# Half of an adaLN modulation as products on TensorE, and the output gate moved into the weights: a hybrid attention and state-space layer on one core

## The chip, the cores and the metric

The kernel runs on one core of one Trainium2 chip. The metric is the device time of one execution in microseconds (us); the runs shown are three. Engines: PE (TensorE, with its weight loads as PEld), DVE (VectorE), ACT (ScalarE), POOL (GpSimd), and SP, whose queue issues most of the transfers. Each engine takes its instructions in the order in which the program holds them. "Line" is a line of the kernel before; lines behind 235 lie 35 to 42 further down in the changed kernel.

## What is computed

One layer on 1024 tokens of width 1024, batch 1, all in float32:

```python
mod = jax.nn.silu(c) @ w_ada + b_ada                 # c: 1024, w_ada: 1024 x 3072
shift, scale, gate = jnp.split(mod, 3, axis=-1)
h = rms_norm(x, norm_g) * (1 + scale) + shift
proj = h @ w_in                                      # 1024 x 2840, split into
q, kcr, vcr, ksl, vsl, kwn, vwn, z_a, g_br, u, z_s = jnp.split(proj, offs, axis=-1)
attn = nsa_attention(...) * silu(z_a)                # 8 heads: compressed, selected, window branch
y = gelu(s5_mixer(u, ...))                           # diagonal state space, 32 groups of 64 states
ssm = y * sigmoid(y @ glu_w + glu_b) * silu(z_s)
mix = jnp.concatenate([attn, ssm], axis=-1) @ w_out  # 1024 x 1024
return x + gate * mix
```

So `shift` and `scale` are needed before any projection, `gate` only at the end, and `gate` runs along the columns of `w_out`.

## The kernel before

The program is a list of named steps in `ORD`; `I(name, *deps)` (line 1348) binds a name to a function and to the steps that must stand ahead of it, and the loop at line 1556 calls them in the order of `ORD`. The framework then lays down each engine's instructions; in the first part VectorE, ScalarE and SP keep the order of the list. `FLG` says on which engine a step's pass runs: "d" VectorE, "p" GpSimd, "a" ScalarE, "t" an accumulating transfer.

Start. `mod_chunk(j)` (line 230) loads 128 columns of `w_ada`, transposed, as 128x1024, multiplies them by silu(c) in one pass `wada<-wada,sc` on VectorE and sums along the row into one column of `macc`. Sixteen chunks make shift (`mb0` to `mb7`) and scale (`ma0` to `ma7`), eight more the gate (`mod0` to `mod7`, later). `mod_cols(k)` turns two sums into the columns `gs`, `sh` of chunk k. `x_block` transposes a chunk of the scaled x into PSUM (`ptr`), `h_chunk` (line 290) writes it as a high part `hhi` and a float32 copy `hf` on ScalarE, and the low part `hlo`. All projections are three products of high and low parts of h and the weights: `TProj` (`kva0` to `kva7`, PSUM `ptp`, weights `wsp` loaded as `wraw`) and `c_proj` (PSUM `pcp`; `pu` for the S5 input, weights `wh`, `wl`).

Middle (50 to 300 us): key, value, query projections, S5 passes, compression. From 300 to 440 us: the first four tiles of 128 queries, eight heads each (scores `S`, probabilities `pp`, their float16 high and low parts `hl`, transposed by SP's DMA transposes into `PT`, products with V in `po`), between the products of the z paths.

End (from 440 us): the GLU writes the S5 branch into `ps`; `gate_row` (line 1026) spreads the gate over 128 partitions; `wout` (line 1035) loads a block of `w_out` as `wor` and splits it into `wo`. `ssm_out(i)` (line 1063) multiplies the S5 half of tile i by its rows of `w_out`, and for each half of 512 columns VectorE makes two passes: PSUM times 0.125 times gate, and an add of x (`xo`; for tile 2 GpSimd's queue adds x by a transfer). Between them run the tiles 7, 6, 5, 4 of the attention. `attn_out` and `last_out` end in `out_half` (line 1306), again two passes: `o<-po,gate` and `o<-o,ps`, and the store.

## Time and profile before

| | |
|---|---|
| Runs | 694.77, 694.79 and 696.99 us, median 694.79 |
| Profiled execution | 691.38 us, of which the span (first to last instruction) is 689.5 us |
| Mean granted clock of TensorE | 0.980 of full speed |
| Busy, PE / DVE / ACT / POOL | 623.5 / 567.3 / 377.9 / 148.6 us |
| Transfers | 116.76 MB, mean 169 GB/s |

Durations below come from the one profiled execution. A busy PE counts any time in which a product is under way, so products with gaps in their flow count too. The chain of waits follows the last instruction back, at each step to what released it.

### The profile page before, as it was taken

What the parts mean: (1) busy time and instruction counts of PE and PEld (TensorE: products, weight loads), DVE (VectorE), ACT (ScalarE), POOL (GpSimd) and SP (SyncE); (2) the same over time, 40 slices, a digit from 0 to 9 for tenths busy, and PEclk for the clock granted to TensorE, in tenths of its full rate; (3) what the DMA queues carried; (4) which work ended last, traced back from release to release, by engine and by line L of the source; (5) the groups of instructions that cost most, each with busy time, mean ns of one, the idle gap of its engine ahead of it and who ended that gap; (6) DMA issues with size and microseconds to landing.
All of it is one profiled execution on the core that took longest, in us unless ns stands there. A gap on an engine that the chain in (4) does not pass through costs nothing.

```text
span 689.5 us, 12618 instructions
## 1 busy us (share of the span) xinstructions
PE 623.5 (90%) x4662; PEld 492.1 (71%) x4662; DVE 567.3 (82%) x1106; ACT 377.9 (55%) x732; POOL 148.6 (22%) x159
## 2 busy tenths in 40 slices
PE   2478999999698999999999999989899999799996
PEld 0356787788587886888788887556677777687775
DVE  5998999777937889876677787998898998998872
ACT  3677413735162252555586786547756855756640
POOL 0153209147232020640011101132001220011010
PEclk9989999999899999999999999999999999999999
DMA  8975211355276624373656868499689599688994
GB/s 319 417 246 104 47 62 41 115 158 136 64 246 199 212 68 109 83 231 94 131 139 154 207 186 183 124 207 208 183 172 206 132 226 222 184 215 213 224 222 86
DMA packets 209759, 116.76 MB, mean 169 GB/s; under 512 B 159073, under 2 KB 188513, under 8 KB 209698
## 3 DMA queue, kind: packets, MB, share of 16 engines
q1 hardware_dynamic: 205858, 109.38, 61.5%
q0 software_dynamic: 3840, 6.57, 4.0%
q8 instruction: 37, 0.61, 0.3%
q14 instruction: 24, 0.20, 0.1%
HBM read 58.10 MB, written 18.61 MB: 111 GB/s over the span
## 4 chain that ended last, share of the span: by engine, by line
PE 41%; DVE 21%; issue 5%; ACT 4%; DMA 2%; SPq 1%; POOL 1%; DVEq 0%; ACTq 0%; POOLq 0%
PE pcp L351 9%; PE po L1053 8%; PE S L1170 7%; DVE hl L148 4%; PE po L1263 3%; PE pglu L1015 3%; DVE st L1187 3%; PE ptp L331 2%; PE ptp L332 2%; PE ptp L330 1%; DVE ps L151 1%; ACT pp L1203 1%; DVE z L151 1%; PE pg L530 1%; PE ph L901 1%
## 5 line engine op out<-in xcount | busy, mean ns | idle before, releaser
L1203 ACT ACTIVATE pp<-S,st 128x640 f32<-128x640 f32 (+7 forms) x128 | 88.6, 699 | 60.5 <-DVE st L1187 46.5
L148 DVE SCALAR_TENSOR_TENSOR hl<-pp,st,hl 128x640 f16<-128x640 f32 (+7 forms) x128 | 100.5, 817 | 4.9 <-ACT hl L1222 4.8
L1222 ACT ACTIVATE hl<-pp,st 128x640 f16<-128x640 f32 (+7 forms) x128 | 85.2, 728 | 8.2 <-DVE st L151 7.1
L1053 PE MATMUL po<-wo,oh 128*128 128x512 f32 x264 | 85.2, 407 | 3.7 <-DVE wo L151 2.4
L351 PE MATMUL pcp<-hhi,wh 128*128 128x512 f32 x208 | 84.8, 408 | 0.0
L351 PE MATMUL pcp<-hhi,wl 128*128 128x512 f32 x208 | 82.6, 397 | 0.0
L351 PE MATMUL pcp<-hlo,wh 128*128 128x512 f32 x208 | 82.4, 396 | 0.0
L1187 DVE TENSOR_REDUCE st<-S 128x1 f32<-128x1024 f32 (+3 forms) x64 | 57.5, 916 | 6.9 <-PE S L1170 6.7
L1170 PE MATMUL S<-kT,qh 128*128 128x128 f32 (+3 forms) x192 | 60.7, 375 | 1.0 <-ACT pp L1203 0.7
L1053 PEld LDWEIGHTS po<-wo,oh 128*128 128x128 f32 x264 | 48.7, 191 | 14.9 <-DVE wo L151 3.8
L330 PE MATMUL ptp<-wsp,hhi 128*128 128x512 f32 x128 | 53.5, 420 | 6.5 <-ACT hhi L296 4.1
L1263 PE MATMUL po<-V,PT 128*128 128x64 f16 x1584 | 59.0, 193 | 0.0
L1263 PEld LDWEIGHTS <-PT 128*128 128x128 f16 x1584 | 54.0, 98 | 5.7 <-issue 5.1
L1170 PE MATMUL S<-kT,ql 128*128 128x128 f32 (+3 forms) x192 | 55.3, 346 | 0.1
L332 PE MATMUL ptp<-wsp,hlo 128*128 128x512 f32 x128 | 53.0, 416 | 1.5 <-POOL hlo L151 1.5
L331 PE MATMUL ptp<-wsp,hhi 128*128 128x512 f32 x128 | 53.5, 418 | 0.5 <-DVE wsp L151 0.5
L151 POOL TENSOR_TENSOR qr<-ropeb 128x512 f32<-128x512 f32 x16 | 23.5, 1488 | 121.7 <-DVE ropeb L151 69.7
L1053 PE MATMUL po<-wo,ol 128*128 128x512 f32 x120 | 47.9, 402 | 0.8 <-DVE ol L151 0.8
L1170 PEld LDWEIGHTS S<-kT,qh 128*128 128x128 f32 x192 | 33.7, 193 | 17.2 <-issue 11.8
L351 PEld LDWEIGHTS pcp<-hlo,wh 128*128 128x128 f32 x208 | 39.1, 188 | 9.2
L351 PEld LDWEIGHTS pcp<-hhi,wh 128*128 128x128 f32 x208 | 39.2, 189 | 8.3
L351 PEld LDWEIGHTS pcp<-hhi,wl 128*128 128x128 f32 x208 | 39.2, 188 | 8.1
(327 smaller groups left out, 1351.5 us busy)
## 6 DMA issues: line engine op xcount, KB each, us to landing
wada<-in_w_adaT_dram SPq DMA_DIRECT2D x24, 512.0 KB, 6.6
wr<-in_w_in_dram SPq DMA_DIRECT2D x14, 512.0 KB, 4.5
x<-in_x_dram SPq DMA_DIRECT2D x8, 512.0 KB, 6.8
wor<-in_w_out_dram SPq DMA_DIRECT2D x8, 512.0 KB, 4.5
out_dram<-o SPq DMA_DIRECT2D x16, 256.0 KB, 2.5
wraw<-in_w_in_dram SPq DMA_DIRECT2D x15, 256.0 KB, 4.7
xo<-in_x_dram SPq DMA_DIRECT2D x14, 256.0 KB, 3.4
ud<-U SPq DMA_DIRECT2D x4, 512.0 KB, 3.2
```

Source lines behind the costliest of these rows:

```text
L148: dve.scalar_tensor_tensor(out=o, in0=a, scalar=s, in1=b, op0=o0, op1=o1, **kw)
L151: e.tensor_tensor(out=o, in0=a, in1=b, op=op)
L330: pe.matmul(p, H(k)[:, tsl], w[:, 0, :], start=k == 0, stop=False)
L331: pe.matmul(p, H(k)[:, tsl], w[:, 1, :], start=False, stop=False)
L332: pe.matmul(p, H(k, True)[:, tsl], w[:, 0, :], start=False, stop=k == 7)
L351: pe.matmul(p[:], w[:, k, :], H(k, l)[:, halves(half)], start=(k == 0 and w is hi and not l), stop=(k == 7 and l))
L1053: pe.matmul(p, a[x][:, k, :], w[y][:, halves(n)], start=k == 0 and m == 0, stop=k == 3 and m == 2)
L1170: pe.matmul(R[:, c0:c1], w, x, start=bank not in opened, stop=False, skip_group_check=True)
L1187: dve.tensor_reduce(out=st[br], in_=us[br][0][:, :W], axis=AX.X, op=OP.max, negate=True)
L1203: act.activation(pp[:, :W], R[:, :W], AF.Exp, bias=st[br], accum_out=st4[:, 1, 2 * (h % 2) + br:2 * (h % 2) + br + 1])
L1222: act.activation(hl[:, :W], pp[:, :W], AF.Copy, scale=st[br])
L1263: pe.matmul(o, p, v, start=first, stop=end, skip_group_check=True)
```

## The change

Four things change. (1) Columns 0 to 511 of shift and scale (chunks k = 0 to 3) come from TensorE: `w_ada` is laid out as two groups of 128x4096, loaded in four pieces of 512 KB each (`wan`), and 16 products with one stationary column of silu(c) and 512 moving columns sum into a row `pga`; the row is copied and turned into four columns by four small products (`pgc`), and one or two passes write `gs` or `sh`. Chunks 4 to 7 stay as they were. (2) `gate_row` comes before the first heads, and `wprep(k)` loads each of the eight blocks of `w_out`, multiplies it by the gate (six on VectorE, two on GpSimd) and writes it to a DRAM tile `wd`; `wout` loads from there. (3) `ssm_out` and `out_half` leave PSUM in one pass each; x is loaded for all tiles. (4) `ORD` and `FLG` are new.

```diff
 ORD = """
-sc1 sc0 lb pu xl_0 sq0 sq2 sq1 sq3 ma7 mb4 ma0 rstd0 mb0 kvaw0 ma5 xl_1 xsc0 sq5 xb10 sq4 xb00 sq6 sq7 mg mc0 h00 mb2
+sc1 scT lb mg gl00 xl_0 sq2 gl10 gl11 sc0 sq1 gl01 sq3 ga00 ga10 ga01 gl02 ga02 sq0 gl03 ga03 rstd0 xsc0 gc0 ga11 gl12
...
+    sc2 = macc[:, 0:16].rearrange("p (a k) -> p a k", a=2)[:, :, 0:4]
+    def sc_cols():
+        cT = w2([128, 2, 4], F32, "cT")
+        dma(cT[:].rearrange("p a k -> p (a k)"), t["cT"])
+        act.activation(sc2, cT[:], AF.Tanh, scale=0.5)
+        stt(sc2, sc2, 1.0, cT[:], OP.add, OP.mult)
+    def ada_load(g, q):
+        GR[g, q] = w = w4([128, 2, 512], F32, "wan")
+        dma(w[:].rearrange("p a n -> p (a n)"), t["w_adaN"][g, :, 1024 * q:1024 * q + 1024], "m")
+    def ada_mms(g, q):
+        if q == 0:
+            GR[g] = ppv("pga")
+        w = GR.pop((g, q))
+        for m in range(2):
+            k = 2 * q + m
+            pe.matmul(GR[g][0:1, :], macc[:, k + k // 4 * 4:k + k // 4 * 4 + 1], w[:, m, :], start=k == 0, stop=k == 7)
+    def ada_cols(g):
+        row = w2([1, 512], F32, "row")
+        act.copy(row[:], GR.pop(g)[0:1, :])
+        p = ppv("pgc")
+        for n in range(4):
+            pe.matmul(p[:, n:n + 1], row[0:1, n * 128:(n + 1) * 128], ident[0:1, 0:1], start=n == 0, stop=n == 3, skip_group_check=True)
+        if g:
+            stt(sh[:, 0:4], p[:, 0:4], 0.5, bada[:, 0:4], OP.mult, OP.add)
+        else:
+            tt(dve, gs[:, 0:4], p[:, 0:4], hng[:, 0, 0:4], OP.mult)
+            tt(dve, gs[:, 0:4], gs[:, 0:4], hng[:, 1, 0:4], OP.add)
...
+    wd = [dram.tile([128, 1024], F32, name=f"wd{k}") for k in range(8)]
     def gate_row():
-        M["gate"] = gate = cur["f2"].tile([128, 1024], F32, name="gate")
+        M["gate"] = gate = w4([128, 1024], F32, "gate")
...
+    def wprep(k):
+        w = w4([128, 1024], F32, "wog")
+        dma(w[:], t["w_out"][128 * k:128 * k + 128, :], "o")
+        tt({"p": pool, "d": dve}[FLG.get(f"wg{k}", "d")], w[:], w[:], M["gate"][:], OP.mult)
+        dma(wd[k][:], w[:], "W")
     def wout(half, k):
...
-            dma(raw[:], t["w_out"][r0:r0 + 128, :], "o")
+        dma(raw[:], wd[4 * half + k][:], "o")
...
-            stt(ps[:, i, halves(n)], p[:], 0.125, M["gate"][:, halves(n)], OP.mult, OP.mult)
-            on = FLG.get(f"xa{i}", "d")
-            if on != "t":
-                xo = f2([128, 512], F32, "xo")
-                dma(xo[:], xr[:, i, halves(n)], "i")
-                tt({"p": pool, "d": dve}[on], ps[:, i, halves(n)], ps[:, i, halves(n)], xo[:], OP.add)
-        if on == "t":
-            pool.dma_start(ps[:, i, :], xr[:, i, :], accum_op=OP.add)
+            xo = f2([128, 512], F32, "xo")
+            dma(xo[:], xr[:, i, halves(n)], "i")
+            stt(ps[:, i, halves(n)], p[:], 0.125, xo[:], OP.mult, OP.add)
...
-        tt(dve, o[:], p[:], M["gate"][:, halves(n)], OP.mult)
-        on = FLG.get(f"ao{i}{n}", "d")
-        if on == "t":
-            pool.dma_start(o[:], r, accum_op=OP.add)
-        else:
-            tt({"p": pool, "d": dve}[on], o[:], o[:], r, OP.add)
+        tt(dve, o[:], p[:], r, OP.add)
...
-            I(f"h{k}{h}", f"mc{k}", f"xb{k}{h}")(
+            I(f"h{k}{h}", *((f"mc{k}",) if k >= 4 else ("gc0", "gc1")), f"xb{k}{h}")(
...
-    I("grow", "sp", "modf")(gate_row)
+    I("grow", "modf")(gate_row)
+    for k in range(8):
+        I(f"wp{k}", "grow", *([f"wp{k - 1}"] if k else []))(lambda k=k: wprep(k))
```

How the instructions stand now, at four places. ScalarE in the first part, before, from its third row on (`x_72` and `x_73` are the halves of x, `hhi_91` the high part of the chunks 0 to 3):

```order
L242 ACTIVATE sq,ss<-x_72 128x1024 x2
L208 CAST wsp<-wraw 128x512
L257 ACTIVATE x_72<-x_72,rstd 128x1024 x2
L242 ACTIVATE sq,ss<-x_73 128x1024 x4
L296 ACTIVATE hhi_91<-ptr,sh,gs 128x512
L296 ACTIVATE hf<-ptr,sh,gs 128x512
L257 ACTIVATE x_73<-x_73,rstd 128x1024 x2
```

And after, from the second copy of a row `pga` on:

```order
L260 COPY row<-pga 1x512
L208 CAST wsp<-wraw 128x512
L331 ACTIVATE hhi_91<-ptr,sh,gs 128x512
L331 ACTIVATE hf<-ptr,sh,gs 128x512
L277 ACTIVATE sq,ss<-x_73 128x1024 x3
L331 ACTIVATE hhi_91<-ptr,sh,gs 128x512
L331 ACTIVATE hf<-ptr,sh,gs 128x512
L292 ACTIVATE x_73<-x_73,rstd 128x1024 x2
L208 CAST wsp<-wraw 128x512
```

The first `hhi` stood behind four squares of the second half of x; now it stands behind one of them, two copies of `pga` and two casts, and three squares stand behind it. From here to the last of three casts `wh<-wr` follow five more passes `hhi` and `hf` of other chunks.

PE's first rows, before:

```order
L224 MATMUL pcb<-cr,ones 128x512 x2
L265 MATMUL ptr<-ident,x_72 128x128 x8
L330 MATMUL ptp<-wsp,hhi_91 128x512
L331 MATMUL ptp<-wsp,hhi_91 128x512
L332 MATMUL ptp<-wsp,hlo_93 128x512
```

And after:

```order
L224 MATMUL pcb<-cr,ones 128x512 x2
L255 MATMUL pga<-wan,macc 1x512 x11
L263 MATMUL pgc<-ident,row 128x1 x4
L255 MATMUL pga<-wan,macc 1x512 x5
L263 MATMUL pgc<-ident,row 128x1 x4
L300 MATMUL ptr<-ident,x_72 128x128 x12
L365 MATMUL ptp<-wsp,hhi_91 128x512
```

The 16 products `pga` and two groups of four small ones now stand ahead of the first transpose of x, and 12 transposes instead of 8 ahead of the first product `ptp`.

SP from 337 us on, when the second tile's probabilities are transposed, before (`wr`, `ad`, `zsd`, `py` are other transfers of that stage):

```order
L1246 DMA_TRANSPOSE PT<-hl 128x4x128 x4
L140 DMA wr_3357<-in_w_in_dram 128x8x128
L140 DMA ad_130<-A 128x512
L140 DMA zsd_125<-zz 128x1024
L140 DMA py__3506<-yd_114 128x512
L1246 DMA_TRANSPOSE PT<-hl 128x4x128 x10
```

And after, at about the same heads:

```order
L140 DMA wog<-in_w_out_dram 128x1024
L1280 DMA_TRANSPOSE PT<-hl 128x4x128 x4
L140 DMA wd_135<-wog 128x1024
L1280 DMA_TRANSPOSE PT<-hl 128x4x128 x4
L140 DMA wog<-in_w_out_dram 128x1024
L1280 DMA_TRANSPOSE PT<-hl 128x4x128 x2
L140 DMA wr_3805<-in_w_in_dram 128x8x128
L140 DMA wd_136<-wog 128x1024
L1280 DMA_TRANSPOSE PT<-hl 128x4x128 x2
```

Loads `wog` and writes `wd` of 512 KB now stand between the transposes; a write waits for its product with the gate, and what is behind it on SP waits too.

VectorE's last rows, before:

```order
L148 SCALAR_TENSOR_TENSOR za<-za,vsc,pat 128x256
L151 TENSOR_TENSOR oh<-za,oh 128x256
L151 TENSOR_TENSOR o<-po,gate 128x512
L151 TENSOR_TENSOR o<-o,ps 128x512
L151 TENSOR_TENSOR o<-po,gate 128x512
L151 TENSOR_TENSOR o<-o,ps 128x512
```

And after:

```order
L148 SCALAR_TENSOR_TENSOR za<-za,vsc,pat 128x256
L151 TENSOR_TENSOR oh<-za,oh 128x256
L151 TENSOR_TENSOR o<-po,ps 128x512 x2
```

Of the two passes of each half one is left.

## Rows read from the trace of the kernel before

**Rows 1.** Stages: us, busy time per engine, PE clock, DMA share, GB/s.

```profile
50.00:300.00 250.00, 234.95 (x1304) 191.81 (x1303) 209.15 (x519) 108.11 (x194) 84.22 (x103) 0.98 0.43 122
300.00:440.00 140.00, 138.47 (x1007) 108.07 (x1006) 104.52 (x199) 93.92 (x246) 19.83 (x20) 1.00 0.65 162
475.00:675.00 200.00, 186.57 (x1960) 151.91 (x1960) 179.94 (x258) 126.19 (x216) 26.25 (x19) 0.98 0.89 199
675.00:689.50 14.50, 8.47 (x127) 6.59 (x125) 3.65 (x6) 0.79 (x2) 0.00 (x0) 1.00 0.30 75
```

**Rows 2.** The chain that ended last, from 475 us on, shares by line.

```profile
by line: PE po L1053 26.5%; PE S L1170 11.5%; DVE hl L148 10.7%; issue 8.6%; DVE st L1187 7.9%; PE po L1263 6.1%; DVE ps L151 3.3%; DVE wo L151 3.2%; DVE o L151 3.2%; DVE ps L148 1.9%; ACT pp L1203 1.9%; DMA PT<-hl 1.7%; DVE za L148 1.4%; A
```

**Rows 3.** Stages of the first 50 us.

```profile
0.00:10.00 10.00, 3.75 (x4) 1.16 (x4) 2.98 (x8) 3.44 (x4) 0.66 (x6) 1.00 0.78 259
10.00:20.00 10.00, 0.00 (x0) 0.00 (x0) 9.02 (x23) 3.13 (x7) 1.27 (x1) 1.00 1.04 406
20.00:30.00 10.00, 5.38 (x15) 3.72 (x16) 8.63 (x26) 7.92 (x13) 1.29 (x1) 1.00 1.03 419
30.00:40.00 10.00, 6.10 (x23) 3.85 (x23) 9.69 (x18) 6.44 (x10) 4.94 (x3) 0.83 1.08 382
40.00:50.00 10.00, 8.29 (x33) 6.09 (x34) 9.05 (x16) 7.48 (x11) 3.39 (x3) 0.83 0.59 181
```

**Rows 4.** VectorE's groups by shape: busy us, mean ns, idle before, releaser.

```profile
L148 DVE SCALAR_TENSOR_TENSOR wada<-wada,sc 128x1024 f32<-128x1024 f32 x24 | 32.6, 1369 | 7.8 <-DMA wada<-in_w_adaT_dram 7.8
...
L151 DVE TENSOR_TENSOR o<-o,ps 128x512 f32<-128x512 f32 x16 | 10.9, 686 | 0.2
...
L151 DVE TENSOR_TENSOR ps<-ps,xo 128x512 f32<-128x512 f32 x14 | 10.2, 732 | 0.1
...
L151 DVE TENSOR_TENSOR wo<-wor,wo 128x1024 fp32r<-128x1024 f32 x8 | 9.6, 1216 | 0.1
```

**Rows 5.** Instructions of the tail in time: start, us, engine and line.

```profile
680.00 0.38 ACT L1279 ACTIVATE A<-po 128x256 f32<-128x256 f32 x1 [6.20 <-PE po L1263]
...
680.91 0.48 DVE L148 SCALAR_TENSOR_TENSOR za<-za,vsc,pat 128x256 f32<-128x256 f32 x1 [6.66 <-PE pat L1333]
...
685.72 0.69 DVE L151 TENSOR_TENSOR o<-o,ps 128x512 f32<-128x512 f32 x1
```

**Rows 6.** GpSimd's groups by shape.

```profile
L151 POOL TENSOR_TENSOR qr<-ropeb 128x512 f32<-128x512 f32 x16 | 23.5, 1488 | 121.7 <-DVE ropeb L151 69.7 <-DVE vs L157 21.9 <-issue 16.4
```

**Rows 7.** Transfers by line: size and us to landing.

```profile
wor<-in_w_out_dram SPq DMA_DIRECT2D x8, 512.0 KB, 4.5
...
PT<-hl SPq DMA_TRANSPOSE x120, 3.5
```

**Rows 8.** The chain that ended last, PE's long pieces.

```profile
445.07 10.37 PE pglu L1015 x24
...
512.26 5.58 PE po L1053 x24
```

**Rows 9.** The start in time.

```profile
2.33 3.75 PE L224 MATMUL pcb<-cr,ones 1*128 1x512 f32 x4 [2.33 <-DMA cr<-in_c_dram]
...
24.97 0.76 ACT L296 ACTIVATE hhi<-ptr,sh,gs 128x512 fp32r<-128x512 f32 x1
...
25.79 0.80 PE L330 MATMUL ptp<-wsp,hhi 128*128 128x512 f32 x1 [2.17 <-ACT hhi L296]
...
50.78 0.73 PE L351 MATMUL pu<-hhi,wh 128*128 128x512 f32 x2 [0.28 <-ACT wh L208]
...
63.74 0.40 PE L330 MATMUL ptp<-wsp,hhi 128*128 128x512 f32 x1
```

**Rows 10.** ScalarE's groups by shape, first 60 us.

```profile
L296 ACT ACTIVATE hhi<-ptr,sh,gs 128x512 fp32r<-128x512 f32 x10 | 7.8, 777 | 7.5 <-PE ptr L265 4.8 <-DVE sh L157 2.2 <-DVE gs L157 0.5
...
L242 ACT ACTIVATE sq<-x 128x1024 f32<-128x1024 f32 x6 | 6.3, 1044 | 2.3 <-DMA x<-in_x_dram 2.3
...
L208 ACT CAST wsp<-wraw 128x512 fp32r<-128x512 f32 x7 | 4.1, 614 | 4.8 <-DMA wraw<-in_w_in_dram 4.8
L208 ACT CAST wh<-wr 128x1024 fp32r<-128x1024 f32 x3 | 3.0, 1038 | 0.0
```

More of the change, by code (lines that the diff above doesn't have):

```diff
@@ L1386, in hymba @@
     I("lb")(lb)
+    I("scT")(sc_cols)
+    for g in range(2):
+        for q in range(4):
+            I(f"gl{g}{q}")(lambda g=g, q=q: ada_load(g, q))
+            I(f"ga{g}{q}", f"gl{g}{q}", "scT", *([f"ga{g}{q - 1}"] if q else []))(lambda g=g, q=q: ada_mms(g, q))
+        I(f"gc{g}", f"ga{g}3", "mg")(lambda g=g: ada_cols(g))
     I("mg", "lb")(mod_gains)
@@ L1572, in arrange @@
     a["w_adaT"] = g("w_ada").T
+    a["w_adaN"] = np.stack([np.ascontiguousarray(g("w_ada")[:, o:o + 512]).reshape(8, 128, 512).transpose(1, 0, 2).reshape(128, 4096)
+                            for o in (1024, 0)])
+    a["cT"] = g("c").reshape(8, 128).T
     a["b_ada"] = g("b_ada").reshape(24, 128).T
```

89 lines of the change are left out of this document (43 added, 46 removed).

## The prediction, made before the changed kernel was run

> **What bounds the kernel now.** I read the table of stages first [rows 1]. In each stage compare PE's busy time with the length of the stage, then VectorE's. From 300 to 440 us PE is busy for 138.47 of 140 us (98.9%): nothing taken off another engine there is worth anything. From 475 to 675 us PE is busy for 186.57 of 200 us (93.3%) and VectorE for 179.94 (90.0%): two engines near their limits that wait for each other, with 13.4 us of idle PE. The tail from 675 us has PE busy for 8.47 of 14.5 us. From 50 to 300 us PE is idle for 15.05 of 250 us. Second, the chain of waits from 475 us on [rows 2]: PE's products lead it, but VectorE's passes are links too, among them `ps` on L151 (3.3%) and `o` on L151 (3.2%), which are the passes at issue. Third, the first 50 us in steps of ten [rows 3]: PE is busy for 23.52 of 50 us, and between 10 and 40 us the DMA engines are full (share 1.03 to 1.08, near 400 GB/s). PE waits there for the weights of the modulation, and for VectorE, which reduces them and is busy for 9.69 us between 30 and 40 us.
>
> **The change part by part.**
>
> *Adds removed.* Each of the 16 half tiles of the last stage loses one add `o<-o,ps`, and 14 of the 16 halves of `ssm_out` lose `ps<-ps,xo`; the multiply that stays turns into the add, in one pass of the same shape. By the groups of VectorE [rows 4] this is 16 x 0.686 = 11.0 us and 14 x 0.732 = 10.2 us, 21.2 us together, all behind the GLU. (The two halves of tile 2 exchange one accumulating transfer of GpSimd's queue for two loads on SP, priced at nothing: such loads are there for the other 14.) What that is worth I take in two ways. (a) Compare stages: from 300 to 440 us VectorE is 74.7% busy and PE 98.9%; from 475 to 675 us 90.0% and 93.3% [rows 1]. So 15.3 points of VectorE go with 5.6 points of PE, 0.37 points per point. Two of the adds lie in the tail; the other 28 are 19.8 us of 179.94. With 160.1 us of VectorE and a stage of 194.5 us its share is 82.3%, PE's share by that slope 96.1%, and 186.57 / 0.961 = 194.1 us: it closes at about 194, a gain of 6. (b) Count in the chain: `ps` and `o` on L151 are 6.5% of the 214.5 us from 475 us to the end, 13.9 us [rows 2]. All `o` on L151 are two passes per half, of which one goes, so half of 3.2% counts, 3.4 us. In `ps` on L151 a part belongs to the GLU product, which stays; if two thirds are the adds, 4.7 us. That is 8 us. In the tail the last add (685.72, 0.69 us) stands behind the last multiply with nothing beside it [rows 5] and goes whole: 0.7 us. I take 7 us with the tail. Bounds: 0, if other waits end last in the same places, and 13.4 + 1.4 = 14.8 us, if all idle PE of the stage and two passes of the tail go.
>
> *Gate into the weights.* `wprep` adds eight products of 128x1024, six on VectorE and two on GpSimd, and 16 transfers of 512 KB. The nearest row of VectorE is `wo<-wor,wo` of that size, 1.216 us [rows 4]: 7.3 us more between about 300 and 400 us, where VectorE is 74.7% busy. They lie beside PE's z products; uncovered they would cost 7.3 us. On GpSimd, two passes of 128x512 with fp32 operands take 2 x 1.488 us [rows 6], so some 3 us for each product, on an engine that is busy for 19.83 of 140 us. `gate_row` with its eight transposes and two copies only moves, from the stage with idle PE into one without; I put 1 us on that. The transfers add 8.4 MB to 140 us at 162 GB/s, 22.7 MB [rows 1]: 37% more, or the share 0.65 turned to 0.89. A load of 512 KB lands after 4.5 us, a transpose of probabilities after 3.5 us [rows 7]. Each write of `wd` waits on SP for its product, and SP holds the transposes of P behind it, for which PE waits in turn. I take nothing for these waits beside the 1 us, as the order has several products of z ahead of them on PE; bounds 0 and 8 us (eight writes, each late by 1 us).
>
> *Modulation on TensorE.* Eight passes `wada<-wada,sc` go from VectorE's first 45 us, 8 x 1.369 = 11 us [rows 4]. The bytes are the same, so what the DMA sets stays. New are 16 fp32 products with 512 columns, and a rule that no first chunk of `h` starts before both halves of four columns are done; before, chunk 0 needed two weight chunks. On PE a fp32 product of 512 columns is two records. At the high clock 24 records took 10.37 us [rows 8], 0.43 us each; the four of `pcb` took 3.75 us at the low one, 0.94 each [rows 9]. The first `wan` chunk ends at 2.7 MB of traffic (2.1 of x and 0.1 of small loads stand ahead of its 0.5). With 2.6 MB in the first 10 us and 4.1 MB in the next ten [rows 3] that is 10.2 us, and the eighth (6.75 MB) is in at 20.2 us. If PE is at the high level behind the first two products, the 32 records take 4 x 0.94 + 28 x 0.43 = 15.8 us and end at 26.0 us: PE, not the DMA, sets this end. The column step (copy, transposing products, a pass of VectorE) is like 680.00 to 681.39 us in the tail, 1.4 us [rows 5], and half a microsecond of the first group's step lies inside: 28 us. So the first `hhi` comes 3 us later than today's 24.97 [rows 9].
> Then it has to be made up. In the new order ACT has nine `hhi`/`hf` (0.775 us), three squares and two scalings (about 1.04), one cast of 0.61 and three of 1.04 us up to the third `wh` [rows 10], 15.9 us, and I add 2.5 us of waits for `rstd1` and its PSUM tiles, an estimate: 46.5 us. The first product of `pu` starts there against 50.78 today [rows 9]. Today 12 more products of `ptp` are done by then, 12 x 0.233 us by the row of 24 in 5.58 us [rows 8], 2.8 us. Ahead by 1.5 us there; behind it PE has 54 products up to k=4, 12.6 us, and some 3 us of transposes and waits for ACT, an estimate. Both orders have the same products ahead of k=4, which starts at 63.74 us today [rows 9] and at about 62 us by this count. I take a gain of 2 us, with bounds of +6 (the first 45 us of VectorE were the wait) and -12 (the low clock, below).
>
> *The rest of the order* from 50 to 300 us: PE is idle for 15 us, which is the upper bound of a gain; a loss of the same size in waits for S5 can't be ruled out. The S5 passes on VectorE start at much the same time by my count (they follow the same casts), so I take 0, with 4 us to either side.
>
> **Sum.** -7 (adds, with the tail) + 1 (middle) - 2 (start) + 0 = -8 us. The profiled execution spans 689.5 us and was timed at 691.4; the median of the runs is 694.8, 3.4 above it. The difference is carried over: 681.5 us of span, 683.4 profiled, 686.8 as a median. I say 686.5.
>
> **The rivals.**
> *Low clock at the start (ends slower).* Each pair of `pga` products waits for a transfer of its own. If PE stays at 1.2 GHz through the `pga` products, the 32 records take 30.1 us instead of 15.8, the columns come at 42 instead of 28 us, and everything behind them on ACT shifts, since the order keeps ACT's `hhi` in line: 14 us lost, 700.5 us. It decides once the products end behind about 38 us. For it: PE's granted clock fell to 0.83 in the mean between 30 and 50 us, when PE was busy for 6 to 8 of 10 us [rows 3]. Against it: PE would have its next chunk waiting at any time after 12 us, as each pair takes longer (1.7 us at the high level) than the transfer of its chunk (1.3 us at 406 GB/s).
> The Trainium skill ("TensorE: Matmul & The Clock Gate", "Loop structure matters more than you think") warns of just this form, a wait for a DMA between products, after which PE runs cold; by that rule the time is the 700 us of this rival. Trace and rule agree on the fall between 30 and 50 us, but no row before shows products of this shape, so the chance stays small.
> *The writes hold up SP (no gain).* The 16 transfers and the waits for products delay transposes from 300 to 440 us by the 8 us of the bound; 686.5 + 7 = 693.5 us. For it: SP issues in order, and the share of DMA rises to 0.89. Against: from 475 us on the share is 0.89 as well, and PE still gets 93.3% [rows 1].
> *VectorE was the whole wait.* Idle PE in the last stage goes to a third: a gain of 13.4 x 2/3 + 1.4 = 10.3 us there, 4 at the start, and 3 from the middle, where S5 starts earlier: 694.8 - 17.3 + 1 = 678.5 us. For it: VectorE is 90% busy and its passes come right behind one another. Against: 600 to 675 us is also full of scores that wait for ACT.
> *The adds were hidden anyway.* The removed passes ran while PE worked; the gain is the tail's 0.7 and the start's 2: 693 us.
>
> **Chances.** Forecast (681 to 692) 0.50; low clock 0.13; SP 0.12; all of VectorE 0.17; hidden 0.08. A difference below 0.3% (2.1 us) can't be told from none here. Faster: 0.48 of the forecast, 0.17, and a third of SP and hidden, 0.07: 0.72. Same: 0.02 + the rest of these two, 0.13: 0.15. Slower: 0.13. The range takes in the forecast, VectorE's case and the lower part of the low clock: 675 to 698.
>
> **What would show it.** In the trace after: VectorE some 15 us below its old busy time from 475 us to the end and PE at 96% there; no passes `o<-o,ps`; the last copy out one pass earlier. At the start: 32 `pga` records with a spacing near 0.43 us, ending at about 26 us, the first `hhi` near 28 us and `pu` near 46.5. From 300 to 440 us PE still at 98% or more. I am wrong if the `pga` records are spaced by more than 0.8 us, if PE's share from 300 to 440 us falls below 96%, or if PE's share from 475 us on stays at 93%.

## The result, and the profile after

The changed kernel takes 701.2 us (median of 16 runs, 696.7 to 704.3) where the kernel before takes 694.8 (16 runs, 690.8 to 697.0): ratio 1.0088, 95% interval 1.0064 to 1.0113. It is slower by 0.9%. The prediction was 686.5 us, range 675 to 698.

The profiled execution of the changed kernel spans 701.7 us, 12.2 more than that of before. To see where they come in, take five events that both kernels have and read their start times from the groups of instructions of each tile: the first score product (`S`), the last product of the z columns (`pcp`), the last GLU product (`pglu`), the last pass that takes a half of the S5 output out of PSUM (`ps<-po`) and the last pass that writes a result (`o`). All are in us; "again" is a second profile of the same kernel.

```
                      before   again   after   again   before -> after   predicted
start to first S       299.5   300.7   307.3   309.0        +7.8          -2 + 0
first S to last pcp    121.3   120.5   131.5   131.0       +10.2          +1
last pcp to last pglu   52.5    53.8    54.2    54.5        +1.7           0
last pglu to last ps   114.7   113.3   105.8   105.5        -8.9       } -7 in both
last ps to last o       97.7    97.8    98.8    98.8        +1.1       }
```

The lines of the first score product and of the last z product, before and then after:

```profile
L1170 PE MATMUL S<-kT,qh x192: 220/395/776, 299.5 to 656.4; 128*128 128x512 f32 x88, 128*128 128x128 f32 x56, 128*128 128x256 f32 x24, 128*128 128x384 f32 x24
...
L351 PE MATMUL pcp<-hlo,wh x208: 392/396/477, 105.5 to 420.8; 128*128 128x512 f32 x104
```

```profile
L1204 PE MATMUL S<-kT,qh x192: 220/392/735, 307.3 to 668.2; 128*128 128x512 f32 x88, 128*128 128x128 f32 x56, 128*128 128x256 f32 x24, 128*128 128x384 f32 x24
...
L386 PE MATMUL pcp<-hlo,wh x208: 387/396/480, 105.0 to 438.8; 128*128 128x512 f32 x104
```

The second profiles repeat every stretch within 1.7 us. But the profiled executions differ by more than the kernels do: they were timed at 691.4 us (3.4 under the median of before) and 703.5 us (2.3 over the median of after), 12.1 us apart, where the medians are 6.4 apart; the second ones, at 691.8 and 704.6 us, lie on the same sides. So the table holds some 6 us that the medians don't have. From the first score to the timed end each kernel takes nearly the same in its two profiles (391.9 and 391.1 us before, 396.2 and 395.6 after). If that also holds at the medians, the first score comes at about 303.3 us before and 305.3 after, an estimate: a loss of about 2 us there and not 7.8. The section on how far one profile can be trusted comes back to this.

The gain is there, in the place where it was expected. One loss far beyond what was expected comes ahead of it, from 300 to 440 us, and one before 300 us whose size is open.

The stages of the changed kernel, which answer to [rows 1] (same columns):

```profile
50.00:300.00 250.00, 232.23 (x1274) 191.09 (x1273) 208.06 (x497) 108.47 (x195) 90.49 (x108) 0.97 0.46 129
300.00:440.00 140.00, 131.22 (x942) 104.30 (x941) 103.81 (x204) 83.97 (x220) 23.04 (x21) 1.00 0.73 180
475.00:675.00 200.00, 187.34 (x1997) 151.22 (x1996) 172.33 (x237) 129.97 (x224) 29.31 (x21) 0.99 0.93 206
675.00:701.70 26.70, 20.36 (x224) 16.12 (x222) 9.51 (x15) 4.12 (x8) 0.00 (x0) 1.00 0.62 137
```

Take the second row first: PE was busy for 138.47 of 140 us before and is now for 131.22 (93.7%). That is the stage in which nothing was to be lost, and below the 96% that the prediction named as a sign of being wrong. The last two rows can't be compared with [rows 1] directly, since everything comes 19 us later. Aligned on the last GLU product, before and then after:

```profile
473.50:588.50 115.00, 107.67 (x1154) 87.71 (x1153) 105.75 (x148) 76.17 (x129) 16.07 (x12) 0.99 0.89 184
588.50:689.50 101.00, 88.88 (x939) 71.89 (x938) 78.33 (x118) 51.88 (x91) 10.18 (x7) 0.98 0.80 195
```

```profile
493.50:599.50 106.00, 101.89 (x1070) 83.30 (x1069) 95.72 (x131) 74.64 (x126) 16.62 (x12) 1.00 0.95 195
599.50:701.70 102.20, 91.11 (x1024) 74.83 (x1022) 70.95 (x103) 52.88 (x95) 7.45 (x6) 1.00 0.85 198
```

VectorE falls from 184.08 to 166.67 us in the two together. PE's share rises from 93.6 to 96.1% in the first and from 88.0 to 89.1% in the second.

VectorE's groups that answer to [rows 4]: the adds are gone, eight of the 24 modulation passes too, and the one-pass results and the weight products have come.

```profile
L148 DVE SCALAR_TENSOR_TENSOR wada<-wada,sc 128x1024 f32<-128x1024 f32 x16 | 22.3, 1391 | 6.2 <-DMA wada<-in_w_adaT_dram 6.0 <-DMA wraw<-in_w_in_dram 0.3
...
L151 DVE TENSOR_TENSOR o<-po,ps 128x512 f32<-128x512 f32 x16 | 11.0, 690 | 10.2 <-PE po L1092 10.2
L148 DVE SCALAR_TENSOR_TENSOR ps<-po,xo 128x512 f32<-128x512 f32 x16 | 10.8, 684 | 1.9 <-DMA xo<-in_x_dram 1.4 <-PE po L1092 0.4
...
L151 DVE TENSOR_TENSOR wog<-wog,gate 128x1024 f32<-128x1024 f32 x6 | 7.3, 1221 | 4.1 <-DMA wog<-in_w_out_dram 4.1
```

The start, which answers to [rows 9] (start, us, engine and line, operation, idle time before it and what ended it):

```profile
10.87 12.32 PE L255 MATMUL pga<-wan,macc 128*1 128x512 f32 x22 [4.69 <-DMA wan<-in_w_adaN_dram]
...
24.10 4.45 PE L255 MATMUL pga<-wan,macc 128*1 128x512 f32 x10
...
30.89 0.78 ACT L331 ACTIVATE hhi<-ptr,sh,gs 128x512 fp32r<-128x512 f32 x1 [1.21 <-PE ptr L300]
...
47.38 0.51 PE L386 MATMUL pu<-hhi,wh 128*128 128x512 f32 x1 [2.10 <-ACT wh L208]
```

The first row is one stretch without idle time behind its start, so of all modulation products only the first waited for its transfer. Its first six records follow one another at 0.81 to 0.85 us (10.87 to 15.94 us), near the pace of `pcb` (0.94 us a record, [rows 9]); from 16.6 us on the records start 0.43 us apart, the pace of the high level, and the last ten take 4.45 us. The granted clock reads 1.00 at both paces, so here the pace and not that column tells the level. The products end at 28.5 us; the first `hhi` is at 30.9 and `pu` at 47.4, against 28 and 46.5 predicted. The first 50 us as a whole, before and then after (columns of [rows 1]):

```profile
0.00:50.00 50.00, 23.52 (x73) 14.82 (x74) 39.37 (x87) 28.41 (x42) 11.55 (x13) 0.93 0.90 330
```

```profile
0.00:50.00 50.00, 35.09 (x109) 15.39 (x110) 26.56 (x65) 27.08 (x41) 7.78 (x10) 0.97 0.91 333
```

PE is busy for 11.6 us more: the new products fill idle time that was there, and VectorE is busy for 12.8 us less.

The first loss, 100 to 150 us. PE's longest waits between 98 and 180 us, in total, times and longest, before and then after:

```profile
PE pvv L824 <- DMA s5X<-ud: 1.2, 1, 1.2
PE pw L795 <- ACT Kt L785: 0.5, 1, 0.5
```

```profile
PE pvv L859 <- DMA s5X<-ud: 8.4, 1, 8.4
```

The first S5 scan (`pvv`) waits for the transfers of its input, `s5X`. SP's own queue shows why they are late, before and after:

```profile
111.79 5.22 SPq L140 DMA_DIRECT2D s5T<-Kt  x8
117.06 3.43 SPq L140 DMA_DIRECT2D s5X<-ud  x7
120.59 0.61 SPq L140 DMA_DIRECT2D kTd<-kh  x1
```

```profile
116.62 5.21 SPq L140 DMA_DIRECT2D s5T<-Kt  x8
121.93 0.60 SPq L140 DMA_DIRECT2D kTd<-kh  x1
122.57 4.14 SPq L140 DMA_DIRECT2D s5X<-ud  x7
```

`s5X` stands behind the eight writes of `s5T`, which wait for VectorE to finish `Kt`: at 111.4 us before, at 116.3 us after. In the trace four passes that prepare the second S5 set (`tc`, `td`, `s5W`, `tc`) stand ahead of `Kt` on VectorE, where two did before, and some passes beside them are longer (`wl<-wr,wh` 2.08 us against 1.24, `skip` 1.39 against 0.27). The scan's input had been sent out at 93.1 us already, 7.7 earlier than before (100.8), and lay there. After this pause PE restarts at the lower of its two clock levels: the granted clock is 0.50 from 128 to 132 us and 1.00 again from 135 us on (1.00 throughout before), and the 16 `pvv` products take 3.63 us against 2.02. The last `pvv` product comes at 255.0 us against 256.2 before, so S5 does not keep the delay to its end; but other products were moved behind it, so this does not tell what of the 8.4 us reaches the first score.

The second loss, 300 to 440 us. SP now waits for the weight products as well (waits of SP's queue, 290 to 439 us):

```profile
SPq L140 <- POOL wog L151: 9.5, 2, 5.8
...
SPq L140 <- DVE wog L151: 2.2, 2, 1.4
```

and PE, which waited for no transfer there before, waits for transposes (PE, 300 to 460 us):

```profile
PE po L1297 <- DMA PTc<-hlc: 2.3, 2, 1.9
PE pqr L1130 <- POOL qr L151: 1.9, 1, 1.9
PE po L1297 <- DMA PT<-hl: 1.9, 3, 1.0
PE pc L1148 <- ACT qc L1145: 1.8, 1, 1.8
```

From the first score to the last z product PE is idle for 8.8 us, and for 1.3 us before. Of the 8.8, 4.2 us are waits for transposes (`PTc`, `PT`) and 3.7 for the query side (`qr`, `qc`). From these two views alone one would say: the writes hold SP, SP holds the transposes, the transposes hold PE. The experiments don't bear that out.

### The profile page after: what moved, and what is told of

Same layout as the page of the kernel before. It is cut to its first block, busy times and chain, and to the rows that moved or that the text cites. A ratio compares the mean times of both kernels' runs of the same rounds, so it can differ in the third digit from the quotient of the medians.

```text
span 701.7 us, 12747 instructions
## 1 busy us (share of the span) xinstructions
PE 639.5 (91%) x4710; PEld 496.8 (71%) x4710; DVE 548.9 (78%) x1058; ACT 378.9 (54%) x735; POOL 155.7 (22%) x164
## 4 chain that ended last, share of the span: by engine, by line
PE 19%; DVE 13%; DMA 8%; ACT 7%; issue 4%; SPq 2%; POOL 1%; DVEq 0%; ACTq 0%; POOLq 0%
PE po L1092 7%; PE S L1204 5%; DVE hl L148 3%; ACT pp L1237 3%; DVE st L1221 2%; PE po L1297 2%; PE pcp L386 2%; DMA PTc<-hlc 1%; PE pglu L1050 1%; ACT hl L1256 1%; DMA PT<-hl 1%; PE pc L1148 1%; DMA py__4327<-yd 1%; SPq L140 1%; DMA wor<-wd 1%
## 5 line engine op out<-in xcount | busy, mean ns | idle before, releaser
L365 PE MATMUL ptp<-wsp,hhi 128*128 128x512 f32 x128 | 52.1, 409 | 3.5 <-ACT hhi L331 3.1
L366 PE MATMUL ptp<-wsp,hhi 128*128 128x512 f32 x128 | 52.9, 413 | 0.9 <-POOL wsp L151 0.9
L1204 PEld LDWEIGHTS S<-kT,ql 128*128 128x128 f32 x192 | 36.2, 191 | 6.7 <-DVE ql L148 3.1
```

The source lines that it names most:

```text
L365: pe.matmul(p, H(k)[:, tsl], w[:, 0, :], start=k == 0, stop=False)
L366: pe.matmul(p, H(k)[:, tsl], w[:, 1, :], start=False, stop=False)
L1204: pe.matmul(R[:, c0:c1], w, x, start=bank not in opened, stop=False, skip_group_check=True)
```

## The experiments

Ratios are to runs of the kernel before on the same chip, with 95% intervals. The stretches are those of the table above, each from one profile.

### Each of the three parts by itself, and each left out

The change has three parts that can be undone separately: the start on TensorE (S), the output part with scaled weights and one-pass results (O), and the order of the rest, from the first U results on (R).

`start_only`: S alone.

```
+ORD up to u7m, FLG of h and kw, ada_load, ada_mms, ada_cols: of the change
 the rest of ORD, wprep, wout, out_half: before
```

> The kernel before with the start of the change alone (half of the modulation on TensorE, its places up to the first U results, h and key-weight halves on the engines that the change puts them on); the order after that and the output part as before. Theory A (the new order of the work from 100 us on is what costs): the first S5 products come 0.5 us earlier, so 0 to -2 us, about 694. Theory B (the transfers and the scaled weights in the middle cost): the same, 694. Theory C (the 16 us of products added to TensorE, the busiest engine, are only partly covered by its idle time at the start, 26.5 us before and 14.9 after): +4 to +5 us, about 699.

`out_only`: O alone, its steps put into the old order behind the same neighbours.

```
 ORD of before, but
-... sp hc33 ct3 glu00 grow ...
+... cmpK grow ... scalev wp0 ... z0_3 wp1 ... hb00 wp2 ... hs07 wp3 ... z3_3 wp4 ... hb12 wp5 ... ha22 wp6 ... z5_5 wp7 ...
```

> The kernel before with the output part alone: gate multiplied into the output weights in the middle through device memory, results taken from PSUM in one pass; the gate row and the eight weight steps stand in the old order behind the same neighbours as in the changed kernel. Theory A (order): the gain of 7 us that the removed additions give stays, about 688. Theory B (the 24 transfers and eight multiplications in the middle hold the attention up by the 11 us lost there in the changed kernel): -7 + 11 = +4, about 699. Theory C (start): 688.

`order_only`: R alone.

```
 ORD up to u7m: before
+ORD from there: of the change, without wp0 to wp7, grow behind glu00; its flags qw7, so3, at6
```

> The kernel before with the changed kernel's order of parts from the first U results on (its gate row where it was), both other edits undone. Theory A (order): the 7.5 us that the first S5 part loses by 148 us, and most of the 11 us lost from 300 to 440 us, come back here: +10 to +18 us, 705 to 713. Theory B (transfers): only the S5 part, and that is regained in part by 225 us: 0 to +7, about 698. Theory C (start): about 695.

`start_out`: S and O, old order.

```
 the edits of start_only and out_only together
```

> Both edits of the code, the order from the first U results on as before, with the gate row and weight steps put in. Theory A (order): -7 -0.5, about 687, faster than both kernels. Theory B (transfers): about 698. Theory C (start): 688 + 5 = 693.

`after_oldout` (S and R) and `after_oldstart` (O and R), the two that complete the set:

```
after_oldout:   wprep, wout, ssm_out, out_half of before; grow behind glu00, no wp steps
after_oldstart: ORD up to u7m and mod_chunk(0..3, 8..11) of before, no ada steps
```

> The changed kernel without its output part: the start on TensorE and the new order stay; gate row after the attention's z work, result in two passes, no scaled weights. Theory F (the order table is fitted to its own code: each part costs in an order that was made for another, and the output part is a gain in its own): 695 + 15 (order alone) + 3 (start alone) = 713, that is 12 us slower than the changed kernel. Theory G (the output part loses in any order, 8 us in the middle by the landmarks of the changed kernel against the one without the device-memory way): about 695, faster than the changed kernel.

> The changed kernel with the old start: all modulation sums on VectorE up to the first U results. Theory F: the new order was fitted to the new start; 701 to 709, no gain. Theory H (the start costs what it costs alone, 2.7 us, since VectorE builds the S5 tables 4 us later and the first scan waits 6 to 8 us): 698.

Measured:

```
                    ratio   interval            to S  S-pcp  pcp-glu  glu-ps  ps-o
start_only    S     1.0039  1.0020 to 1.0057   307.8  120.7   52.3   113.3    97.8
out_only      O     1.0686  1.0638 to 1.0733   306.1  147.3   55.4   121.6   103.9
order_only    R     1.0254  1.0185 to 1.0324   303.8  124.5   55.6   111.3   106.8
start_out     SO    1.0661  1.0609 to 1.0712   309.4  145.4   53.9   122.0   100.8
after_oldout  SR    1.0210  1.0176 to 1.0245   302.1  124.2   55.4   111.0   107.4
after_oldstart OR   1.0091  1.0052 to 1.0130   306.0  131.9   53.1   105.7    98.1
after         SOR   1.0088  1.0064 to 1.0113   307.3  131.5   54.2   105.8    98.8
```

Theory A (the order loses) and Theory B (the output part loses) both hold in part, and none had the size of `out_only` (741.4 us). Theory C's +4 to +5 us for the start were too much, the 0 to -2 of the others too little: it is +2.7. `start_out`, expected between 687 and 698 us, took 740.1. Theory G (the output part loses in any order) falls. What stands is Theory F: the parts don't add up. The output part costs 6.9% in the order of before, with its steps in the one placement that was tried, and gains in the new one, 1.0088 / 1.0210 = 0.988 and, without the start, 1.0091 / 1.0254 = 0.984. The new order without the output part costs 2.1 to 2.5%; more than half of that is the tail, 107 us instead of 98. What makes that tail longer is open. The second pass of each result, which the output part takes away, is not enough: `o` makes 9.0% of the chain that ended last from 593 us on in `after_oldout`, 10.0 us, and 6.7 and 9.0% of the tails of before in its two profiles, 6.8 and 9.2 us. What that chain has and those of before don't have is 7.7 us (6.9%) of a transfer, `A<-ad`. The start is worth nothing with the rest (1.0088 against 1.0091) and costs 0.4% alone. For `order_only` Theory A had 705 to 713, measured 709.7; `after_oldout` was expected at 713 and took 708.3; `after_oldstart` came out at 698.0, which Theory H (698) had.

`start_only` has the start as its only edit, and shows what becomes of it. PE's longest wait between 98 and 180 us there:

```profile
PE pkt L515 <- POOL kr L152: 5.5, 1, 5.5
```

`kr` is two passes of GpSimd behind VectorE's `ropeb`. They start at 105.44 us (104.00 before) and take 8.02 us (3.96 before), so 1.4 us of the wait come from the later start and 4.1 from the longer passes; what makes them longer is open. VectorE does eight passes less, but it was not the amount of its work that counted. From 20 to 30 us VectorE is busy for 0.94 of 10 us in the changed kernel (8.63 in [rows 3]), since no chunk of `h` can start before 30.9, and from 87.5 to 112.5 us it is as full as before (25.00 us in `start_only`, 24.93 before). VectorE's first pass on the loaded S5 parameters is at 56.6 us (55.6 before), but `s5x<-s5p`, a few passes on, is at 65.5 us against 60.8.

### The middle: is it SP's queue, the transfers or the weights' lateness?

`out_wpool` and `after_wpool` issue the eight writes from GpSimd's queue; `out_local` and `after_local` have no way through device memory.

```
out_wpool, after_wpool:
-DQ = {"y": ...}
+DQ = {"y": ..., "W": pool}
out_local, after_local:
-    dma(raw[:], wd[4 * half + k][:], "o")
+    dma(raw[:], t["w_out"][r0:r0 + 128, :], "o")
+    tt(pool, raw[:], raw[:], M["gate"][:], OP.mult)
 and no wprep; gate_row behind sp, as before
```

> As the output part alone in the old order (741 us), but the eight writes of scaled weights are issued from GpSimd's queue. Theory Q (on SP's queue each write waits for its multiplication, 29 us in all between 270 and 440 us, and the transposes of the softmax rows and the loads behind it wait with it): most of the +47 us go, 690 to 700. Theory T (the 24 transfers of 512 KB and the multiplications themselves take the room): stays at 735 to 745. Theory L (the weights come too late at the end of the way, wor from device memory ended waits of 5.2 and 5.3 us in the chain): 730.

> The output part in the old order without the way through device memory: the gate row stands where it stood before, each weight tile is loaded, multiplied by it on GpSimd (2.4 us each) and split; results leave PSUM in one pass. Theory Q: nothing is left that holds SP's queue, so the gain of the removed additions shows: 686 to 690. Theory T: the same, 688. Theory L: each weight tile is 2.4 us later, and the first product waits for it: 690 to 695. A fourth, that the removed additions were hidden anyway: 694 or more.

> The changed kernel with the eight writes issued from GpSimd's queue. Theory Q: SP waited 11.7 us for the multiplications there between 270 and 440 us; -6 to -10 us, 691 to 695. Theory T: 701, as it is. Theory L: 701.

> The changed kernel without the way through device memory: gate row where it was before the change, gate multiplied on GpSimd behind each load of a weight tile. Theory Q and Theory T: the 11 us lost from 300 to 440 us come back in part, 690 to 695. Theory L: 2.4 us later weights, 698. If the loss there is the order's alone: 701.

```
               ratio   interval            to S  S-pcp  pcp-glu  glu-ps  ps-o
out_wpool     1.0504  1.0437 to 1.0571   306.2  139.3   58.2   118.7   103.3
out_local     1.0307  1.0263 to 1.0351   304.2  120.5   53.8   125.9   105.8
after_wpool   1.0134  1.0081 to 1.0186   304.2  134.6   53.3   105.5    98.1
after_local   1.0217  1.0173 to 1.0261   305.1  123.8   55.7   112.4   105.5
```

Theory Q (SP's queue) falls for the changed kernel: with the writes on another queue the stretch from S to the last z product takes 134.6 us, not less than 131.5, PE waits as long for transposes (4.3 us against 4.2), and the time doesn't improve. In the old order the queue accounts for 8 of 26 us (147.3 to 139.3). `out_wpool` took 730.7 us, the number of Theory L (730), but not for its reason: 18 us of its loss lie from S to the last z product, ahead of the place where late weights could hold PE. `out_only`'s SP had waited as the changed kernel's does, only longer (SP, 270 to 440 us):

```profile
SPq L140 <- POOL wog L151: 20.5, 2, 14.8
...
SPq L140 <- DVE wog L151: 8.8, 3, 5.1
```

With the whole of it out of the stretch (`after_local`, `out_local`) the stretch is at 123.8 and 120.5 us. So 7.7 of the 10.2 us lost there belong to the scaled weights, and the other 2.5 to the order (124.2 in `after_oldout` too). A us or two of such a split can't be told from none: `after_s5first` below, which moves three names near 100 us, has 128.8 us there instead of 131.5. But the loss only moves: the last two stretches take 218 and 232 us instead of 204.6, and the two kernels take 709.7 and 715.9 us, more than any theory had but, for `out_local`, the open-ended fourth. Theory L is right in part: in `after_local` PE waits 5.8 us for `wo` from 485 us on (0.2 in the changed kernel), in `out_local` 3.5 us from 478 us on, beside 10.9 us for transposes. The rest is not traced. `out_local` shows a price of the one-pass result that the prediction did not have: it reads x, so it can't leave PSUM before x has landed (VectorE's waits, 478 to 715 us):

```profile
DVE ps L147 <- DMA xo<-in_x_dram: 5.8, 2, 5.5
```

Before, the first pass freed PSUM without x. In the changed kernel the same wait is 1.4 us in all (the group of `ps<-po,xo` above).

### The first scan's wait, and the tiles

`after_s5first` moves three names; `before_n17` takes two of the shared 4 KB tiles from the kernel before.

```
after_s5first:
-mats0 kpat0 prep1 xl0 tab0 scan0
+mats0 xl0 kpat0 tab0 scan0 prep1
before_n17:
-N4, N2, F2 = 19, 13, 6
+N4, N2, F2 = 17, 13, 6
```

> The changed kernel with one edit of the order: the first scan and the load of its input stand before the second set's preparation, so that VectorE finishes the first Toeplitz columns (Kt) ahead of six operations of the second set. Theory H (the 8.4 us that TensorE waits there for s5X reach the end): the first S5 product at about 124 instead of 129 us, 696 to 698. Rival (what is lost at 129 us is made up by 225 us, where the landmark of the changed kernel is level with before): 701.

> The kernel before with 17 instead of 19 of the 4 KB tiles that all stages share, nothing else changed. Theory R (gate row and scaled weights hold two or three of the 19 tiles from 264 to 405 us, so the z weights are loaded later: that, not the transfers themselves, is what costs in the middle): 30 us between 300 and 440 us as in the old order with the output part, 715 to 725. Rival (the transfers and multiplications cost, tiles are plenty): 694 to 698.

`after_s5first`: 700.9 us, ratio 1.0123 (1.0055 to 1.0190), no faster than the changed kernel. The scan's first product does come at 125.4 instead of 129.1 us, but the second set is late in turn: the first output product is at 149.7 us (148.0 in the changed kernel) and PE waits 3.8 us for `kr` and 2.3 for `s5W`. The rival is right: moving one wait made another, and the 8.4 us are not to be had by that.

`before_n17`: ratio 1.0225 (1.0192 to 1.0258), 708.7 us. With nothing added but two tiles less, S to the last z product takes 131.0 us, 9.7 more than before and the same as in the changed kernel (131.5); the other stretches are 305.5, 53.8, 114.8 and 97.7. Theory R had 30 us for that stretch and 715 to 725 in all, its rival 694 to 698: the time lies between the two. Theory R's way from the tiles to PE is late loads of z weights. These loads, the last three in SP's queue (before, `before_n17` and the changed kernel):

```profile
343.13 0.52 SPq L140 DMA_DIRECT2D wr<-in_w_in_dram  x1
...
366.58 0.57 SPq L140 DMA_DIRECT2D wr<-in_w_in_dram  x1
...
380.90 0.58 SPq L140 DMA_DIRECT2D wr<-in_w_in_dram  x1
```

```profile
357.38 0.53 SPq L140 DMA_DIRECT2D wr<-in_w_in_dram  x1
...
382.19 0.57 SPq L140 DMA_DIRECT2D wr<-in_w_in_dram  x1
...
396.21 0.53 SPq L140 DMA_DIRECT2D wr<-in_w_in_dram  x1
```

```profile
359.08 0.38 SPq L140 DMA_DIRECT2D wr<-in_w_in_dram  x1
...
382.71 0.52 SPq L140 DMA_DIRECT2D wr<-in_w_in_dram  x1
...
397.26 0.38 SPq L140 DMA_DIRECT2D wr<-in_w_in_dram  x1
```

They come 14 to 16 us late in both, nearly at the same times; measured from the first score, 8 to 10 us late. But no wait of PE in that stretch is for z weights. In `before_n17` PE's waits are for `qc` (3.7 us) and `pp` (3.3), and the granted clock is 0.96 instead of 1.00; in the changed kernel they are for transposes, `qr` and `qc`, as above. In the changed kernel the gate row holds one of the 19 tiles from its copy out of PSUM (272 us) to the last product (404), and each weight another. That two tiles are worth 10 us in that stretch is shown; by which wait they cost it is not, and that they are what costs in the changed kernel is a guess, since fewer tiles also shift other instructions.

### Multiplications or transfers, and a version without either in the middle

```
after_smallmul:
-    tt(..., w[:], w[:], M["gate"][:], OP.mult)
+    tt(..., w[:, 0:4], w[:, 0:4], M["gate"][:, 0:4], OP.mult)
after_nodma:
-    dma(w[:], t["w_out"]...) ; tt(..., w[:], w[:], gate) ; dma(wd[k][:], w[:])
+    tt(..., w[:], gate, gate)
after_pre: gate_row behind glu00; wprep keeps its tile, no wd:
-    dma(wd[k][:], w[:], "W")
+    M["wog", k] = w
+... qr7 wp4 ... hc35 wp5 ... hs71 wp6 ... ub33 wp7 ... so4 wp0 ... so5 wp1 ... so7 wp2 ... so6 wp3 ...
mix_pre: the same, old start, ORD of before up to kt
```

> The changed kernel with each of the eight multiplications of output weights cut from 1024 to 4 columns (so most of the gate is left out): transfers, tiles and waits stay, 6 x 1.22 us of VectorE and 2 x 2.40 us of GpSimd go. Theory R (the tiles that gate and scaled weights hold are what costs from 307 to 439 us): 699 to 701. Theory M (the multiplications, in the way of VectorE's softmax work and of the writes behind them): 692 to 695.

> The changed kernel without the 16 transfers in the middle: the eight tiles are taken and a multiplication of the same size (gate by gate, used by nothing) is done in each, and the output weights are loaded plain later (so the gate is left out). Theory R: tiles are still held, but for a shorter time, since no load or write holds them: 696 to 699. Theory T (the 16 transfers of 512 KB, 8.4 MB beside the transposes): the whole 8 to 11 us between first S and last z product go, 690 to 693. Theory M: 701.

> The changed kernel with the scaled weights made later and kept in SBUF: gate row after the z work, four weight tiles loaded and multiplied on GpSimd from 450 us on and four among the S5 output rows, nothing written to device memory. Theory R and T: first S to last z product falls from 131 to 124 us, and the gain of the one-pass results stays: 690 to 694. If GpSimd's multiplications and the later tiles slow the attention as they did where they stood right behind the load: 700 or more.

> The same late scaling, with the old start and the old order up to the key-table load at about 290 us, and the changed kernel's order from there: first S at 300 us as before, then 382 to 390 us as in the changed kernel less its middle: 682 to 690, faster than both. Theory F (an order does well only with the parts that it was made with): 700 or more.

```
                 ratio   interval            to S  S-pcp  pcp-glu  glu-ps  ps-o
after_smallmul  1.0100  1.0032 to 1.0168   303.4  130.6   55.6   105.8    98.6
after_nodma     1.0065  1.0032 to 1.0098   305.9  127.7   52.0   105.6    98.0
after_pre       1.0402  1.0327 to 1.0478   303.1  123.8   62.6   116.5   107.0
mix_pre         1.0353  1.0275 to 1.0431   303.6  125.4   63.7   116.7   107.0
```

The multiplications' length is worth 1 us of the stretch (131.5 to 130.6): Theory M falls. Without the 16 transfers it is 4 us shorter (131.5 to 127.7): Theory T has half of what it claimed. The transfers don't go alone, though: without them each tile is also held for a shorter time, and Theory R's 696 to 699 us for that (697.6 measured) and 699 to 701 for `after_smallmul` (700.3) both came out. So transfers and the hold on tiles are not told apart here. Another 4 us, from 127.7 to the 123.8 of `after_local`, go only when tiles and multiplications leave the stretch as well. With 2.5 us of the order that makes up the 10.2.

The versions that scale late (`after_pre`, `mix_pre`) have the stretch at 124 and 125 us, as expected, and lose more behind it: 62.6 to 63.7 us to the last GLU product, 11 us in the S5 output and 8 in the tail. The 690 to 694 us expected of `after_pre` (720.7 measured) and the 682 to 690 of `mix_pre` (716.6) were far off; the old order up to 290 us did not even bring first S back to 300 (303.6). No kernel of this study is faster than the one before.

### How far one profile can be trusted

```
before_again, after_again: no edit
```

> The kernel before, unchanged, profiled a second time: how far do the landmarks of one execution move? The first profile's own time, 691.4 us, was 3 us under the median of its runs, and kernels whose code is the same up to 260 us started the first scores 4.7 to 6.6 us later than it. If that profile was an early one, first S comes at 302 to 305 us here and the end at 690 to 695; if the order of the other kernels is what moved them, first S is at 299 to 300 again.

> The changed kernel, unchanged, profiled a second time. If the stretches read from its first trace stand: first S at 305 to 308 us, last z product 131 us later, last result from the S5 part 106 us after the last product of the gated unit. If they are one execution's accident, they differ by more than 3 us.

First S is at 300.7 and 309.0 us, and the stretches stand in the first table: the same kernel repeats them within 1.7 us. But `out_local`, where PE has the products of before in the same order up to the output part at 480 us, reached first S at 304.2. So some 4 us before 300 us come with a program or with one execution of it, and not with the order there. Which of the two stays open: the expectation took the second profile of before for a test of this, but that execution, at 691.8 us, was as early as the first. In all runs with the old start and the old order up to 260 us first S lies between 299.5 and 306.2 us, with the new start and the new order up to there between 302.1 and 309.0. The two overlap, and the 7.8 us of the first table are not shown to belong to the change. The stretch behind it repeats better (S to the last z product 121.3, 120.5 and 120.5 in the three).

## Why the prediction was wrong, step by step

*Adds removed, -7.* Right as a number, and in part by luck. The last two stretches took 212.4 us before and take 204.6: -7.8. VectorE is down by 17 us where 15 were expected, and PE's share in the first of them is 96.1%, as written down; in the second it is 89.1%, and in the stretch that was named, 475 to 675 us, 93.7%, which now starts 18 us before the last GLU product. But the -7.8 is a sum of two that the prediction did not tell apart: the new order without the output part takes 218.4 us there, 6.0 more, and within the new order the output part gives 13.8 us (218.4 to 204.6), near the upper bound of 14.8. The exchange of VectorE's share for PE's by one slope priced neither of the two.

*Middle, +1 with a bound of 8.* This is the step that failed: +10.2 to the last z product, and 11.9 with the next stretch, beyond the bound. The term that was wrong is the one for waits: nothing was taken for them, "as the order has several products of z ahead of them on PE". PE waits for 8.5 us in this stretch, 4.2 for transposes and 3.7 for the query side, against 1.2 us before. The mechanism named for the bound, writes that hold up SP and its transposes, is not what decides: on another queue nothing came back. The scaled weights as a whole are worth 7.7 us and the order 2.5; of the 7.7, half went with the transfers and the shorter hold on tiles, half with the rest. What of it acts on PE stays open. The step left out that the new work takes tiles: two tiles less cost before 9.7 us in the same stretch. "PE 98.9% busy" says that PE hardly waits there today, not that it can't be made to.

*Start, -2.* The times in it were nearly right (products to 28.5 instead of 26.0 us, `hhi` 30.9 instead of 28, `pu` 47.4 instead of 46.5), and the products at k=4 came at 62.4 us against 63.7, about as written down. The conclusion was wrong: by the first S5 matrix (`pk`, 101.7 against 102.2 us, and 103.3 in the second profile of each) half a microsecond of it or nothing was left, and alone the start costs 0.4%.

*The rest of the order, 0 with 4 to either side.* Wrong in its mechanism, the sentence that the S5 passes on VectorE start at much the same time. The first does (55.8 against 55.6 us), but the ones behind it don't keep up: `s5x<-s5p` is at 64.8 instead of 60.8 us, `Kt` comes 4.9 us later and the first scan waits 8.4 us. What reaches first S is open: 7.8 us by the profiles, about 2 by the estimate from the medians. The start and the order together were to give -2, so 4 to 10 us are missing here.

*The rivals.* The low clock held for the first six records, where four were counted, and not for the others: the products end at 28.5 us, far from the 38 that the rival needs. The Trainium skill ("TensorE: Matmul & The Clock Gate", "Loop structure matters more than you think") would have products run cold when they wait for a transfer in between. The modulation products don't test that, since only the first of them waited. Where PE did wait for a transfer, 8.4 us for `s5X`, the trace agrees: a granted clock of 0.50 and `pvv` products at nearly half the pace. "The writes hold up SP" had the right place and 8 of the 10.2 us, but by a mechanism that did not bear out, and it ended at 693.5 us since all else was left as forecast. The adds were not hidden, with 7.8 us gained at the end, and S5, which "VectorE was the whole wait" had earlier, came later. No rival had a loss ahead of 300 us but the low clock; waits for S5 were named in the step on the order, as a loss that can't be ruled out, and given no chance of their own.

*The sum* was made of separate terms: -8 us against +6.4 by the medians, of which the middle and the stretch behind it account for 11, the start and the order for about 4 by the estimate, and the end, 0.8 better than forecast, takes a little back. All seven combinations of the three parts are slower than before, and the sign of the output part turns with the order: that is the deeper failure. The order of each kernel is a list of some 700 names fitted to its own waits, and a term priced in the old order is not the term in the new one.

## What to carry to other kernels

Where a list of names fixes the order, price an edit together with the order it comes with: the same edit measured +6.9% in one order and -1.2% in the other. A stage in which PE is 99% busy is not safe from new work off PE: ask what that work takes (tiles, a place in a queue) and who needs it. Work taken from an engine counts only if its successors start earlier; the 12.8 us that VectorE was less busy in the first 50 us did not shorten the kernel. And before a profile's stretches are added up to a difference between two kernels, compare its own time with the median of the runs.

## What the runs showed of the hardware

PE's products of 512 columns with one weight column, behind 4.7 us without work and then without a gap, started 0.85 us apart for six records and 0.43 us apart from then on. 8.4 us without work at 121 us were followed by `pvv` products at 3.63 us for 16 instead of 2.02, with a granted clock of 0.50 from 128 to 132 us.

VectorE's passes can be slower beside GpSimd's: in `out_local`, where GpSimd multiplies the weights, VectorE's `wo<-wor,wo` takes 1.75 us in the median and up to 3.26 (1.22 and 1.23 before). Of its eight passes four overlap with a GpSimd pass for half of their time or more and take 2.28 to 3.26 us; a fifth, beside GpSimd for 93% of its time, took 1.21, and the three others 1.22 to 1.23. GpSimd's two `kr` passes at 105 us in `start_only` take 8.02 us against 3.96 before; VectorE was busy throughout in both, so its being busy alone does not explain that.
